# A hybrid decoder block on one core: w_out in program order, its weight tiles split one ahead, the Fox heads gated in pairs, ten modulation blocks within the attention

## The chip, the cores and the metric

One core of a Trainium2 chip runs the whole program. The metric is the device time of one execution in microseconds (us), the median of several. Engines: PE multiplies matrices, VectorE (DVE) and ScalarE (ACT) work element by element, GpSimd (POOL) does a little of the same and issues some DMAs, SyncE (SP) issues the other DMAs from one queue.

## What is computed

One decoder block for 512 tokens and model width 2048, in fp32. A vector c gives six modulation vectors; the hybrid mixer has eight forgetting-attention heads (Fox) and eight native-sparse heads (NSA); their outputs are normalised per group, scaled by beta, joined and multiplied by `w_out`; then comes a SwiGLU feed-forward.

```
mod = silu(c) @ w_ada + b_ada ; sh1, sc1, g1, sh2, sc2, g2 = split(mod, 6)
u   = rmsnorm(h) * (1 + sc1) + sh1 ; z = u @ w_in
y_f = rmsnorm(o_fox(z)) * beta_fox ; y_n = rmsnorm(o_nsa(z)) * beta_nsa
h   = h + g1 * (concat(y_f, y_n) @ w_out)
u   = rmsnorm(h) * (1 + sc2) + sh2
h   = h + g2 * ((silu(u @ w_gate) * (u @ w_up)) @ w_down) ; out = rmsnorm(h)
```

## The kernel before

Tiles have 128 rows. Each fp32 operand is split into a rounded high part and the rest (`wh`, `wl` for weights, `yh`, `yl` for a head's output), and a product is three matmuls (L278 to L280, or L283 to L285 where the activation is the stationary side): high by high, low by high, high by low.

**Weights.** `load_w` takes two rows of weight tiles ("a ct", 2 x 128 rows by 128 to 512 columns) through one ring of three raw tiles `wr`: SP loads it, ACT casts `wh` (L244), VectorE subtracts `wl` (L249). There are two `wh`/`wl` buffers; while there is a spare pool, every third tile goes to a further one, `wx`. `gemm` loads and splits a tile at each ct and then multiplies.

**The sides.** While `gemm` runs, `pump` advances side work by a step at each ct: `ada_block` (a modulation block of 512 columns: eight steps of one 512 KB load `ad` from the same ring of three and two VectorE operations each, L384 and L386; then eight one-column matmuls, L390), attention items (`att.run`) and, in the third and last pass over v, the NSA heads' gating `mix_chunk` (L947): the raw head `or` is reloaded (`reload`, L954, from a ring of five tiles), multiplied by the row scale (L948, on POOL for NSA heads and odd Fox heads, else VectorE), split into `yh` (ACT, L950) and `yl` (VectorE, L951). `mix_hook` pumps one step at ct 1 and two at each later ct. Nine modulation blocks are queued for the attention (L790), three remain.

**w_out.** Sixteen tiles of 128 output columns in groups of 4, 2, 4, 4, 2 columns (`g0`, `g1`, then groups 6, 10, 14, named by their first column). The sum runs over heads 8 to 15 (NSA, ct 0 to 3) and then 0 to 7 (Fox, ct 4 to 7). `g0` and `g1` do ct 0 to 3 first, with the attention's last items; the Fox heads are gated by `fox_hook` (L1024), two at each ct of `g1`; then ct 4 to 7 of `g0` and `g1` and the whole groups 6, 10 and 14 in the loop from L1193. At the end of a group `res_add` (L1061) adds to the residual `hT` and POOL stores it and sums squares. `x_hook` also loads the first feed-forward weights (`w_load`, L1076, `raw`) in group 10 and splits them (`w_sums`, `x_high`, `x_low`, `s_split`) in group 14.

**What sets the order.** SP runs in the program's order throughout. On the other engines a scheduler chooses the order until the feed-forward, where `tc.manual_schedule()` (L1231) makes them follow the program. A first pass, `z_qn` (L727), is followed by a v pass whose first tile `w_v0` is split ahead of the heads' rotations (L743).

Of the kernel before, what the change touches and what calls it, by code (L numbers as in the profile page):

```python
# [79 lines left out]
def hymba_block(ctx: ExitStack, tc: tile.TileContext, x, c, positions, w_ada, b_ada, norm_attn,  # L80
# [1111 lines left out]
    side_ada.extend(ada_block(pf, sec, j) for sec, j in todo_ada[9:])
    for i0, n, g in ((0, 4, g0), (4, 2, g1), (6, 4, BANKS_A), (10, 4, BANKS_B), (14, 2, BANKS_A)):  # L1193
        k0 = 8 if i0 < 6 else 0
        if i0 >= 6:
            g = out_group(i0, n, g)

        def x_hook(ct):
            if ct == k0 // 2 + 2:
# [4 lines left out]
            if i0 == 14:
                if ct == 2:
                    hsum["b"] = bank("s")
                    sum_tok(hsum, hsum["t"], True, False)
                if 1 <= ct < 3:
                    w_sums(ct - 1)
                if 1 <= ct < 4:  # L1210
                    x_high(ct - 1)
                if 1 <= ct < 5:
                    x_low(ct - 1)
                if 3 <= ct < 5:
                    s_split(ct - 3)
                if ct == 5:
                    w_sums(2)

        gemm(*g, order=order, k0=k0, hook=x_hook, n_ada=1)
        res_add(i0, [o[3] for o in g[3]], 2, hsum, "hsum")  # L1220
        for i in range(i0, i0 + n):
            nc.gpsimd.dma_start(hsd[i], hT[i])
# [204 lines left out]
```

## Time and profile before

| | |
|---|---|
| time, 3 runs | 2456.65, 2457.55 (median), 2460.13 us |
| the profiled execution | 2450.92 us, its span 2448.0 us |
| granted TensorE clock, mean | 0.981 of full |
| PE busy | 2355.1 us (96%) |
| VectorE, ACT, POOL busy | 65%, 42%, 14% |

All times below are counted from the span's start. PE is busy nearly throughout, so only its idle time, and the time that it runs at the lower granted clock, can change while its products stay the same. "Half clock" below is a granted clock of 0.50.

### The profile page before, as it was taken

How to read it: one execution, taken by the hardware profiler on the slowest of the kernel's cores; microseconds unless marked ns; L12 is line 12 of the kernel's file. 1: busy time of each engine (PE TensorE's matmuls, PEld its weight loads, DVE VectorE, ACT ScalarE, POOL GpSimd, SP SyncE). 2: the span in 40 equal slices, each digit the busy share in tenths (PEclk: the TensorE clock that was granted, in tenths of full speed). 3: DMA queues.
4: the chain of work that ended last, by engine and by line, in shares of the span. 5: the costliest groups of instructions: out<-in, count | busy, mean ns of one | idle time of the engine just before them, and what ended most of it. 6: DMA issues, size and time to landing. Idle time of an engine off the chain costs nothing.

```text
span 2448.0 us, 38482 instructions
## 1 busy us (share of the span) xinstructions
PE 2355.1 (96%) x14717; PEld 2100.4 (86%) x14717; DVE 1579.6 (65%) x2711; ACT 1016.0 (42%) x1531; POOL 341.5 (14%) x370
## 2 busy tenths in 40 slices
PE   6998999999999989889999999999999999999998
PEld 4677887888888767789999999999999888888887
DVE  6876786887755576596777777777776643333333
ACT  3224544344423332365555555555555422222133
POOL 0003002000001121251222121212221100000010
PEclk8998999999999999999999999999999999999999
DMA  9864743463554277559898989898988644333322
GB/s 332 283 198 147 205 139 95 130 190 117 180 174 129 85 249 253 186 122 237 211 231 215 228 213 232 220 225 212 221 200 193 192 151 141 123 120 121 102 95 101
DMA packets 322713, 440.31 MB, mean 180 GB/s; under 512 B 26224, under 2 KB 217552, under 8 KB 322528
## 3 DMA queue, kind: packets, MB, share of 16 engines
q1 hardware_dynamic: 289104, 348.21, 44.0%
q0 software_dynamic: 31120, 85.45, 18.7%
q10 hardware_dynamic: 2304, 4.20, 0.5%
q8 instruction: 115, 1.88, 0.3%
q14 instruction: 70, 0.57, 0.1%
HBM read 340.18 MB, written 28.38 MB: 151 GB/s over the span
## 4 chain that ended last, share of the span: by engine, by line
PE 54%; DVE 1%; DMA 0%; issue 0%; ACT 0%; SPq 0%; DVEq 0%; ACTq 0%
PE py L1161 12%; PE py L1164 11%; PE py L1163 11%; PE psmm L278 3%; PE psmm L279 3%; PE psmm L280 3%; PE pss L278 2%; PE pss L279 2%; PE pss L280 2%; PE pso L279 1%; PE pso L278 1%; PE pso L280 1%; DMA wr<-in_w_down_dram 0%; PE pso L1058 0%; DVE ul L1141 0%
## 5 line engine op out<-in xcount | busy, mean ns | idle before, releaser
L249 DVE TENSOR_TENSOR wl<-wr,wh 128x1024 fp32r<-128x1024 f32 (+2 forms) x211 | 239.0, 1133 | 381.5 <-ACT wh L244 378.4
L244 ACT CAST wh<-wr 128x1024 fp32r<-128x1024 f32 (+2 forms) x211 | 199.5, 948 | 502.7 <-PE psmm L279 199.7
L1164 PE MATMUL py<-uh,ls 128*128 128x256 f32 x1408 | 397.6, 282 | 3.6 <-DVE ls L1107 3.6
L1163 PE MATMUL py<-ul,hs 128*128 128x256 f32 x1408 | 397.6, 282 | 2.2 <-DVE ul L1141 2.2
L1161 PE MATMUL py<-uh,hs 128*128 128x256 f32 x1408 | 398.4, 283 | 1.0 <-DVE ev L1178 0.5
L1107 DVE TENSOR_TENSOR ls<-sum,hs 128x1024 fp32r<-128x1024 f32 x176 | 215.2, 1223 | 196.5 <-ACT hs L1101 196.5
L1101 ACT CAST hs<-sum 128x1024 fp32r<-128x1024 f32 x176 | 184.5, 1049 | 377.3 <-PE py L1163 257.5
L1163 PE MATMUL py<-ul,hx 128*128 128x256 f32 x1056 | 298.8, 283 | 4.0 <-DVE ul L1141 4.0
L1161 PE MATMUL py<-uh,hx 128*128 128x256 f32 x1056 | 299.3, 283 | 1.7 <-ACT uh L1140 1.4
L1164 PE MATMUL py<-uh,lx 128*128 128x256 f32 x1056 | 298.3, 282 | 0.0
L1164 PEld LDWEIGHTS py<-uh,ls 128*128 128x128 f32 x1408 | 267.0, 190 | 4.7 <-DVE ls L1107 4.6
L1163 PEld LDWEIGHTS py<-ul,hs 128*128 128x128 f32 x1408 | 267.0, 190 | 3.3 <-DVE ul L1141 3.3
L1161 PEld LDWEIGHTS py<-uh,hs 128*128 128x128 f32 x1408 | 267.1, 190 | 2.7 <-DVE ev L1178 1.3
L1097 POOL DMA_DIRECT2D lx<-raw x176 | 156.2, 887 | 580.2 <-ACT lx L1096 419.4
L1163 PEld LDWEIGHTS py<-ul,hx 128*128 128x128 f32 x1056 | 200.8, 190 | 5.1 <-DVE ul L1141 5.1
L1161 PEld LDWEIGHTS py<-uh,hx 128*128 128x128 f32 x1056 | 200.6, 190 | 2.2 <-ACT uh L1140 1.7
L1164 PEld LDWEIGHTS py<-uh,lx 128*128 128x128 f32 x1056 | 200.7, 190 | 0.0
L386 DVE SCALAR_TENSOR_TENSOR acc<-ad,sl,acc 128x512 f32<-128x512 f32 x180 | 141.6, 787 | 43.2 <-DMA ad<-in_w_ada_dram 41.4
L1092 ACT CAST hx<-raw 128x768 fp32r<-128x768 f32 x176 | 144.3, 820 | 11.3 <-DMA raw<-in_w_gate_dram 11.3
L1096 ACT ACTIVATE lx<-raw 128x768 fp32r<-128x768 f32 x176 | 148.1, 841 | 1.8 <-DMA raw<-in_w_gate_dram 1.8
L278 PE MATMUL psmm<-fh,wh 128*128 128x512 f32 x352 | 137.0, 389 | 0.0
L280 PE MATMUL psmm<-fh,wl 128*128 128x512 f32 x352 | 136.9, 389 | 0.0
(441 smaller groups left out, 5284.3 us busy)
## 6 DMA issues: line engine op xcount, KB each, us to landing
lx<-raw POOLq DMA_DIRECT2D x176, 384.0 KB, 5.2
ad<-in_w_ada_dram SPq DMA_DIRECT2D x128, 512.0 KB, 4.1
raw<-in_w_up_dram SPq DMA_DIRECT2D x176, 256.0 KB, 4.2
raw<-in_w_gate_dram SPq DMA_DIRECT2D x176, 256.0 KB, 4.5
wr<-in_w_down_dram SPq DMA_DIRECT2D x88, 512.0 KB, 3.6
ad<-in_w_ada_dram SPq DMA_DIRECT2D x128, 256.0 KB, 6.0
wr<-in_w_in_dram SPq DMA_DIRECT2D x104, 256.0 KB, 3.5
wr<-in_w_in_dram SPq DMA_DIRECT2D x24, 512.0 KB, 4.4
```

The source lines that it names most:

```text
L244: nc.scalar.copy(wh[:, :, sc], v)
L249: nc.vector.tensor_tensor(held[1][:, :, sc], v, split_ap(held[0])[:, :, sc], op=OP.subtract)
L278: nc.tensor.matmul(dst, wh[:, k, w], ah, start=first, stop=False)
L279: nc.tensor.matmul(dst, wh[:, k, w], al, start=False, stop=False)
L280: nc.tensor.matmul(dst, wl[:, k, w], ah, start=False, stop=last)
L1096: nc.scalar.activation(lx[s], raw[s][:, 1:4, :], AF.Copy, scale=-1.0)
L1097: nc.gpsimd.dma_start(split_ap(lx[s]), raw[s][:, 1:4, :], accum_op=OP.add)
L1101: nc.scalar.copy(hs[s], sums[s])
L1107: nc.vector.tensor_tensor(ls[s], sums[s], split_ap(hs[s]), op=OP.subtract)
L1161: nc.tensor.matmul(o, wh[:, wi, js], vh[:, vi, :], start=k == 0 and j == 0, stop=False, skip_group_check=True)
L1163: nc.tensor.matmul(o, wh[:, wi, js], vl[:, vi, :], start=False, stop=False, skip_group_check=True)
L1164: nc.tensor.matmul(o, wl[:, wi, js], vh[:, vi, :], start=False, stop=k == KG - 1, skip_group_check=True)
```

## The change

In the pass after `z_qn` the first two weight tiles are split ahead instead of one. Ten modulation blocks instead of nine are queued for the attention. `mix_hook` pumps one step per ct; what is left is pumped in `g0`. After the attention's last items every engine follows the program (`manual_schedule` begins there, not at the feed-forward). `load_out` loads and splits a tile one ct ahead of its `products`. The Fox heads are gated in pairs (`fox_pair`): four are reloaded at once, both products on VectorE, both `yh`, both `yl`, then the reload of the pair four further on. `res_add` of a group runs after the next group's first ct (`owed`), the first feed-forward weights are loaded at ct 3 to 7 of group 10 and ct 0 of group 14, and their splits are spread over ct 1 to 7 of group 14. Two modulation blocks remain for the loop, at set cts (`n_ada`).

```
-    w_v0 = z_qn(0, lambda: ahead(p_v0, extra=wsm), k0=ND // 2, ...)
+    w_v0 = z_qn(0, lambda: ahead(p_v0, extra=wsm) + ahead(p_v0, 1, extra=wsm), k0=ND // 2, ...)
-    side_ada.extend(ada_block(pa, sec, j) for sec, j in todo_ada[:9])
+    side_ada.extend(ada_block(pa, sec, j) for sec, j in todo_ada[:10])
-            pump(side_mix, 1 if ct == 1 else 2)
+            pump(side_mix, 1)
...
-    gemm(*g0, order=order, n_ada=1, n_att=1.25, k1=8)
+    def load_out(i0, ct):
+        return load_w(p_out[i0], order[2 * ct] // 2)
+    def products(g, ct, w):
+        gemm(*g, order=order, k0=2 * ct, k1=2 * ct + 2, first=[lambda: w])
+    gemm(*g0, order=order, n_ada=1, n_att=1.25, k1=8, hook=lambda ct: pump(side_mix, 2 if ct == 0 else 1000))
+    w1 = [load_out(4, ct) for ct in range(2)]
     att.drain()
-    rb = rows_of(sum_rstd(osum[0], FH * HD, "o", "rsf"), "o", q_tmp("rbf"))
-    def fox_hook(ct):
-        for h in fox[2 * ct:2 * ct + 2]:
-            mix_chunk(reload(h), h, rb)
-    gemm(*g1, order=order, n_ada=1, k1=8, hook=fox_hook)
     pump(side_ada, 1000)
+    ms.enter_context(tc.manual_schedule())
+    fox = {h: reload(h) for h in range(4)}
+    r = sum_rstd(osum[0], FH * HD, "o", "rsf")
+    products(g1, 0, w1[0])
+    rb = rows_of(r, "o", q_tmp("rbf"))
+    w1.append(load_out(4, 2))
+    products(g1, 1, w1[1])
+    def fox_pair(h):
+        for i in (h, h + 1):
+            nc.vector.tensor_tensor(fox[i], fox[i], rb, op=OP.mult)
+        for i in (h, h + 1):
+            y[i] = act_tile("y", i)
+            nc.scalar.activation(y[i][0], fox[i], AF.Copy, scale=beta[:, i:i + 1])
+        for i in (h, h + 1):
+            nc.vector.scalar_tensor_tensor(y[i][1], fox[i], beta[:, i:i + 1], split_ap(y[i][0]), ...)
+        if h + 5 < FH:
+            for i in (h + 4, h + 5):
+                fox[i] = reload(i)
+    fox_pair(0); w1.append(load_out(4, 3)); products(g1, 2, w1[2])
+    fox_pair(2); w0 = [load_out(0, 4)];     products(g1, 3, w1[3])
+    fox_pair(4); w0.append(load_out(0, 5)); products(g0, 4, w0[0])
+    fox_pair(6); w0.append(load_out(0, 6)); products(g0, 5, w0[1])
...
+        for ct in range(c0, 8):
+            if ct < 7:
+                nw = load_out(i0, ct + 1)
+            elif n_grp < 4:
+                nw = load_out(groups[n_grp + 1][0], starts[n_grp + 1])
+            pump(side_ada, ct in n_ada.get(i0, ()))
+            products(g, ct, w)
+            w = nw
+            if ct == c0 and owed is not None:
+                owed()
-            if i0 == 10 and 2 <= ct < 8:
-                w_load(ct - 2)
+            if i0 == 10 and ct >= 3:
+                w_load(ct - 3)
```

**SP around the Fox heads.** SP's queue from the load of `g1`'s ct 2 on, before: `or` are raw heads (from the third pair's first on), `wr` of 128x2x256 are tiles of `g1`, of 128x2x512 tiles of `g0`.

```order
L225 DMA wr_1541_8271<-in_w_out_dram 128x2x256
L956 DMA or_1544_8289<-osp_2480 128x512
L956 DMA or_1547_8296<-osp_2480 128x512
L225 DMA wr_1550_8303<-in_w_out_dram 128x2x256
L956 DMA or_1552_8320<-osp_2480 128x512
L956 DMA or_1555_8327<-osp_2480 128x512
L225 DMA wr_1558_8400<-in_w_out_dram 128x2x512
L380 DMA ad_1562_8407<-in_w_ada_dram 128x2x512
L225 DMA wr_1563_8435<-in_w_out_dram 128x2x512
```

And now, from the same load on:

```order
L225 DMA wr_1543_8280<-in_w_out_dram 128x2x256
L956 DMA or_1550_8308<-osp_2480 128x512
L956 DMA or_1551_8310<-osp_2480 128x512
L225 DMA wr_1552_8312<-in_w_out_dram 128x2x256
L956 DMA or_1558_8339<-osp_2480 128x512
L956 DMA or_1559_8341<-osp_2480 128x512
L225 DMA wr_1560_8343<-in_w_out_dram 128x2x512
L225 DMA wr_1567_8371<-in_w_out_dram 128x2x512
L225 DMA wr_1574_8411<-in_w_out_dram 128x2x512
```

In both, heads 4 and 5 stand before the load of `g1`'s ct 3, and heads 6 and 7 before that of `g0`'s ct 4; now no `ad` stands between the tiles of `g0`, and `g0`'s ct 4, 5 and 6 are called for back to back.

**ACT at the same place.** ACT's instructions from the row scale `rbf` on, before (`yh` is a head's high part, `wh` and `wx` are a weight tile's):

```order
L177 COPY rbf_1520_8199<-pso_1521_8200 128x512
L950 ACTIVATE yh_1527_8228<-or_1526_8225,vec_252 128x512
L950 ACTIVATE yh_1530_8235<-or_1529_8232,vec_252 128x512
L950 ACTIVATE yh_1536_8260<-or_1535_8257,vec_252 128x512
L950 ACTIVATE yh_1539_8267<-or_1538_8264,vec_252 128x512
L244 CAST wh_1542_8273<-wr_1541_8271 128x2x256
L950 ACTIVATE yh_1545_8292<-or_1544_8289,vec_252 128x512
L950 ACTIVATE yh_1548_8299<-or_1547_8296,vec_252 128x512
L244 CAST wx_1551_8305<-wr_1550_8303 128x2x256
```

And now:

```order
L177 COPY rbf_1541_8273<-pso_1542_8274 128x512
L244 CAST wh_1544_8282<-wr_1543_8280 128x2x256
L1046 ACTIVATE yh_1546_8300<-or_1534_8232,vec_252 128x512
L1046 ACTIVATE yh_1548_8303<-or_1535_8234,vec_252 128x512
L244 CAST wx_1553_8314<-wr_1552_8312 128x2x256
L1046 ACTIVATE yh_1554_8331<-or_1536_8236,vec_252 128x512
L1046 ACTIVATE yh_1556_8334<-or_1537_8238,vec_252 128x512
L244 CAST wh_1561_8345<-wr_1560_8343 128x1024
L1046 ACTIVATE yh_1563_8363<-or_1550_8308,vec_252 128x512
```

The cast of `g1`'s ct 2 moved from behind four heads to ahead of all, that of ct 3 from behind six heads to behind two, and that of `g0`'s ct 4 from behind ct 3's to between the second pair and the third. VectorE follows the same pattern.

**SP in group 10.** SP's queue from the first feed-forward weights (`raw`) on, before:

```order
L1080 DMA raw_1656_9084<-in_w_up_dram 128x2x256
L1081 DMA raw_1656_9084<-in_w_gate_dram 128x2x256
L225 DMA wr_1657_9087<-in_w_out_dram 128x2x512
L380 DMA ad_1660_9093<-in_w_ada_dram 128x2x512
L1080 DMA raw_1661_9121<-in_w_up_dram 128x2x256
L1081 DMA raw_1661_9121<-in_w_gate_dram 128x2x256
L225 DMA wr_1662_9124<-in_w_out_dram 128x2x512
L380 DMA ad_1665_9130<-in_w_ada_dram 128x2x512
```

And now, from the load just ahead of them:

```order
L225 DMA wr_1662_9107<-in_w_out_dram 128x2x512
L380 DMA ad_1665_9113<-in_w_ada_dram 128x2x512
L1115 DMA raw_1666_9141<-in_w_up_dram 128x2x256
L1116 DMA raw_1666_9141<-in_w_gate_dram 128x2x256
L225 DMA wr_1667_9144<-in_w_out_dram 128x2x512
L1115 DMA raw_1670_9174<-in_w_up_dram 128x2x256
L1116 DMA raw_1670_9174<-in_w_gate_dram 128x2x256
L225 DMA wr_1671_9177<-in_w_out_dram 128x2x512
```

A modulation load `ad` stood after every weight tile; now the last one stands ahead of the first `raw`.

## Rows read from the trace of the kernel before

**Rows 1.** The page: busy time, share of the span, instructions.
```profile
PE 2355.1 (96%) x14717; PEld 2100.4 (86%) x14717; DVE 1579.6 (65%) x2711; ACT 1016.0 (42%) x1531; POOL 341.5 (14%) x370
```

**Rows 2.** Stretches: us, busy time (count) per engine, granted clock, DMA share, GB/s.
```profile
224.20:234.40 10.20, 6.21 (x24) 5.86 (x25) 9.93 (x14) 5.17 (x11) 4.63 (x3) 0.50 0.42 130
692.66:717.15 24.49, 23.92 (x194) 23.30 (x194) 16.22 (x24) 3.37 (x6) 0.00 (x0) 1.00 0.70 209
779.17:810.45 31.28, 26.58 (x203) 26.08 (x203) 18.04 (x19) 12.10 (x18) 12.67 (x8) 0.89 0.36 119
797.60:804.40 6.80, 4.81 (x22) 4.51 (x22) 4.91 (x6) 2.48 (x4) 1.83 (x2) 0.50 0.35 110
890.68:906.95 16.27, 13.87 (x57) 10.79 (x56) 12.81 (x16) 5.18 (x8) 5.88 (x7) 0.90 0.82 279
906.95:951.54 44.59, 44.06 (x194) 35.95 (x194) 26.47 (x30) 10.64 (x12) 5.57 (x7) 1.00 0.74 244
951.54:1003.28 51.74, 48.20 (x210) 38.38 (x208) 34.68 (x44) 18.46 (x23) 11.46 (x14) 0.97 0.93 288
971.70:975.10 3.40, 3.40 (x9) 2.36 (x8) 3.37 (x6) 2.31 (x3) 0.87 (x1) 0.50 0.93 202
```

**Rows 3.** PE in order of time: start, us, line, [idle before <-releaser].
```profile
226.93 0.61 PE L283 MATMUL psmm<-wh,uh 128*128 128x288 f32 x1 [4.14 <-ACT wh L244]
...
797.40 0.43 PE L283 MATMUL psmm<-wh,uh 128*128 128x256 f32 x1 [2.71 <-ACT wh L244]
800.04 0.58 PE L285 MATMUL psmm<-wl,uh 128*128 128x256 f32 x1 [1.99 <-DVE wl L249]
...
852.13 1.96 PE L175 MATMUL pso<-cs,rsfr 128*128 128x128 f32 x8 [0.89 <-DVE rsfr L169]
859.59 0.50 PE L278 MATMUL pss<-yh,wh 128*128 128x512 f32 x1 [1.97 <-ACT wh L244]
867.59 0.50 PE L278 MATMUL psmm<-yh,wh 128*128 128x512 f32 x1
896.33 0.60 PE L280 MATMUL pss<-yh,wl 128*128 128x512 f32 x1 [2.32 <-DVE wl L249]
```

**Rows 4.** VectorE by form, 692 to 717 us: busy, mean ns of one.
```profile
L386 DVE SCALAR_TENSOR_TENSOR acc<-ad,sl,acc 128x512 f32<-128x512 f32 x15 | 11.3, 751 | 4.9 <-DMA ad<-in_w_ada_dram 4.5
L249 DVE TENSOR_TENSOR wl<-wr,wh 128x512 fp32r<-128x512 f32 x4 | 2.8, 688 | 1.6 <-PE psmm L285 1.0 <-ACT wh L244 0.6
```

**Rows 5.** VectorE, then POOL, in order of time, 786 to 800 us.
```profile
798.24 1.75 DVE L249 TENSOR_TENSOR wl<-wr,wh 128x512 fp32r<-128x512 f32 x1
...
786.76 12.67 POOL L948 TENSOR_TENSOR or<-or,rbn 128x512 f32<-128x512 f32 x8 [19.32 <-ACT rbn L177]
```

**Rows 6.** SP's queue in order of time; a long row is blocked.
```profile
774.76 15.45 SPq L956 DMA_DIRECT2D or<-osp  x2
...
851.64 7.52 SPq L956 DMA_DIRECT2D or<-osp  x2
860.68 0.42 SPq L225 DMA_DIRECT2D wr<-in_w_out_dram  x1
```

**Rows 7.** ACT in order of time at 859 and 866 us.
```profile
858.93 0.60 ACT L244 CAST wh<-wr 128x512 fp32r<-128x512 f32 x1
...
866.49 1.05 ACT L244 CAST wh<-wr 128x1024 fp32r<-128x1024 f32 x1 [2.06 <-DMA wr<-in_w_out_dram]
```

**Rows 8.** DMA issues: count, KB each, us to landing; issued at 858.8, 860.6, 955 to 990.
```profile
wr<-in_w_out_dram SPq DMA_DIRECT2D x1, 256.0 KB, 2.9
...
wr<-in_w_out_dram SPq DMA_DIRECT2D x1, 512.0 KB, 5.7
...
wr<-in_w_out_dram SPq DMA_DIRECT2D x6, 512.0 KB, 7.4
```

**Rows 9.** Who PE waited for in group 10: total, times, longest.
```profile
PE pss L278 <- ACT wh L244: 2.7, 2, 2.1
PE pss L280 <- DVE wl L249: 0.8, 2, 0.5
```

More of the change, by code (lines that the diff above doesn't have):

```diff
@@ L742, in hymba_block @@
     p_v0 = cols2(w_in, C_VS, 512, 2, P)
-    w_v0 = z_qn(0, lambda: ahead(p_v0, extra=wsm), k0=ND // 2, start=ND // 2, first=z_first)
+    w_v0 = z_qn(0, lambda: ahead(p_v0, extra=wsm) + ahead(p_v0, 1, extra=wsm), k0=ND // 2, start=ND // 2, first=z_first)
     nc.sync.dma_start(ca, cst[:, K_CM:])
@@ L1010, in hymba_block @@
         att.step()
-    pump(side_mix, 1000)
     def out_group(i0, n, tags):
         Z = [bank(t) for t in tags[:n]]
-        return [cols(w_out, i0 * P, n * P)], y, ND, [("ws", m * P, P, Z[m]) for m in range(n)]
+        return p_out[i0], y, ND, [("ws", m * P, P, Z[m]) for m in range(n)]
     order = list(range(8, 16)) + list(range(8))
-    g0 = out_group(0, 4, BANKS_A)
-    gemm(*g0, order=order, n_ada=1, n_att=1.25, k1=8)
-    att.drain()
-    rb = rows_of(sum_rstd(osum[0], FH * HD, "o", "rsf"), "o", q_tmp("rbf"))
@@ L1022, in hymba_block @@
-    fox = order[8:]
-    def fox_hook(ct):
-        for h in fox[2 * ct:2 * ct + 2]:
-            mix_chunk(reload(h), h, rb)
-    g1 = out_group(4, 2, BANKS_B)
-    gemm(*g1, order=order, n_ada=1, k1=8, hook=fox_hook)
-    pump(side_ada, 1000)
+    groups = [(0, 4, BANKS_A), (4, 2, BANKS_B), (6, 4, BANKS_A), (10, 4, BANKS_B), (14, 2, BANKS_A)]
+    p_out = {i0: [cols(w_out, i0 * P, n * P)] for i0, n, _ in groups}
+    def load_out(i0, ct):
+        return load_w(p_out[i0], order[2 * ct] // 2)
@@ new lines, in products @@
+    def products(g, ct, w):
+        gemm(*g, order=order, k0=2 * ct, k1=2 * ct + 2, first=[lambda: w])
+    g0 = out_group(*groups[0])
+    gemm(*g0, order=order, n_ada=1, n_att=1.25, k1=8, hook=lambda ct: pump(side_mix, 2 if ct == 0 else 1000))
+    w1 = [load_out(4, ct) for ct in range(2)]
+    att.drain()
+    pump(side_ada, 1000)
+    ms = ExitStack()
+    ms.enter_context(tc.manual_schedule())
+    fox = {h: reload(h) for h in range(4)}
+    r = sum_rstd(osum[0], FH * HD, "o", "rsf")
+    g1 = out_group(*groups[1])
@@ new lines, in hymba_block @@
+    products(g1, 0, w1[0])
[9 more added lines that the diff above has]
+        for i in (h, h + 1):
+            nc.vector.scalar_tensor_tensor(y[i][1], fox[i], beta[:, i:i + 1], split_ap(y[i][0]),
+                                           op0=OP.mult, op1=OP.subtract)
+        if h + 5 < FH:
+            for i in (h + 4, h + 5):
+                fox[i] = reload(i)
@@ L1031, in hymba_block @@
+    fox_pair(0)
+    w1.append(load_out(4, 3))
+    products(g1, 2, w1[2])
+    fox_pair(2)
+    w0 = [load_out(0, 4)]
+    products(g1, 3, w1[3])
+    fox_pair(4)
+    w0.append(load_out(0, 5))
+    products(g0, 4, w0[0])
+    fox_pair(6)
+    w0.append(load_out(0, 6))
+    products(g0, 5, w0[1])
     spare.clear()
@@ L1191, in hymba_block @@
     hsum = {"n": 14}
[L1192 to L1199, printed above, removed]
+    side_ada.extend(ada_block(pf, sec, j) for sec, j in todo_ada[10:])
+    w, owed = w0[2], None
+    starts = [6, 4, 0, 0, 0]
+    n_ada = {4: range(4, 8), 6: range(8), 10: range(4), 14: (2,)}
+    for n_grp, (i0, n, tags_) in enumerate(groups):
+        g = (g0, g1)[n_grp] if n_grp < 2 else out_group(i0, n, tags_)
+        c0 = starts[n_grp]
+        for ct in range(c0, 8):
[8 more added lines that the diff above has]
+                owed()
+            if ct == (7 if i0 == 0 else c0 + 2):
                 for i in range(i0, i0 + n):
                     nc.sync.dma_start(hT[i], xsp[i])
-            if i0 == 10 and 2 <= ct < 8:
-                w_load(ct - 2)
+            if i0 == 10 and ct >= 3:
+                w_load(ct - 3)
             if i0 == 14:
[L1205 to L1213, printed above, removed]
+                if ct == 0:
+                    w_load(5)
+                if ct in (1, 2, 5):
+                    w_sums({1: 0, 2: 1, 5: 2}[ct])
+                if ct in (1, 3, 5):
+                    x_high(ct // 2)
+                if ct in (2, 4, 6, 7):
+                    x_low((2, 4, 6, 7).index(ct))
                 if 3 <= ct < 5:
@@ L1216, in x_hook, with owed @@
                 if ct == 5:
[L1217 to L1222, printed above, removed]
+                    hsum["b"] = bank("s")
+                    sum_tok(hsum, hsum["t"], True, False)
+        def owed(i0=i0, n=n, g=g):
+            res_add(i0, [o[3] for o in g[3]], 2, hsum, "hsum")
+            for i in range(i0, i0 + n):
+                nc.gpsimd.dma_start(hsd[i], hT[i])
+    owed()
     pump(side_ada, 1000)
@@ L1230, in hymba_block @@
     aw.close()
-    ms = ExitStack()
-    ms.enter_context(tc.manual_schedule())
     kk = ExitStack()
```

## The prediction

> **What bounds the kernel now.** The page comes first: PE is busy 96% of the span, the next engine 65% [rows 1]. The change leaves PE's products as they are, so it can only win or lose PE's idle time and the time that PE runs at half clock. The table of stretches [rows 2] shows where there is any in what is touched, PE's own time line [rows 3] what ended each wait: on the matmuls of L278 to L285 always a weight tile's high part from ACT or its low part from VectorE. So each part below asks when a weight tile is split, and before that, when SP could issue its load.
>
> Two numbers serve throughout. A ct of two 128-row tiles costs PE 3.06 us in the v passes (24.49 us for eight [rows 2]) and in `w_out` about 5.4 us at four columns and 2.7 at two (44.59 us, less 0.5 idle and one L390 set, for eight of four columns). And half clock follows some waits: 797.6 to 804.4 (6.8 us) behind one of 2.71 us [rows 3], and 971.7 to 975.1 (3.4 us), are at 0.50 [rows 2]. A stretch of 3.4 us at half clock in which PE is busy gives 1.7 us of work away.
>
> **The first v pass.** Its second tile was cast behind the heads' rotations: PE waited 4.14 us at 226.93 [rows 3] and stood at half clock from 224.2 to 234.4, 10.2 us of which it was busy 6.21 [rows 2]. Split ahead, ct 1 follows ct 0 at once. But the cast and the subtraction (0.6 and 0.7 us) now stand ahead of the third head's rotation, whose later steps delay the third tile's split; VectorE was busy 9.93 of these 10.2 us, so its work, not the tile, ends the stretch. The wait moves from ct 1 to ct 2. I take -0.7 us; bounds -3 (half of the waits and the half clock's 3.1 us go) and +1 (the rotations 1.3 us later, little gained).
>
> **The third v pass, 779.17 to 810.45.** It took 31.28 us where the second took 24.49; with its eight L175 matmuls (0.8) some 6.0 us are lost. SP's queue stood still 15.45 us from 774.76, because two chunks a ct asked for more raw heads than the ring of five had free [rows 6]; the weight loads behind them came late, and PE waited 2.71 and 1.99 us [rows 3] and stood at half clock for 6.8. With one chunk a ct SP isn't blocked so. In return the tenth modulation block stands in this pass: eight loads of 512 KB on the same ring of three, and sixteen VectorE operations of 0.75 us [rows 4]. A ct then asks of VectorE 0.69 (`wl`), 1.5 (block) and 0.75 (`yl`, taken as the block's operation, which has its form) = 2.94 us if nothing slows it. POOL works 12.67 us on eight products, 1.58 each [rows 5], one a ct now, and beside it a `wl` took 1.75 instead of 0.69: over 1.58 us VectorE does about 0.7 us of work, so a ct costs 2.94 + 0.85 = 3.8 us against PE's 3.06. Eight of them are 30.3 us, and with L175's 0.8 this is 31.1: next to nothing. Some of it is hidden by the tiles split ahead: I take -1; bounds -6 (all that was lost) and +1.5 (the ring at 4 us a ct).
> By the Trainium skill (GPSIMD Engine Reference, 8. Key points) GpSimd and VectorE contend only where VectorE reads two SBUF inputs or is in a two-port mode. The block's operations read two, and the 1.75 us agree; were nothing slowed, the pass would need 25.3 us and the term be -6, which is the low bound anyway.
>
> **The attention's end.** `g1`'s ct 0 no longer fills the last items' waits but stands behind them, where it covers the row scale's chain (the 0.89 us wait at 852.13 [rows 3]). Work and cover trade places: 0, with L175 some 1.2 us later (twelve matmuls of 0.23, as 2.7 us a two-column ct, from 850.5 on end at 853.3).
>
> **The Fox heads.** This is the largest term, and it is a loss. SP's order is the same in both kernels: heads 4 and 5, `g1`'s ct 3, heads 6 and 7, `g0`'s ct 4. Head 5 waits for head 0's raw tile to be free, head 7 for head 2's (a ring of five). Before, all four `yl` of heads 0 to 3 came in one run, and `g0`'s ct 4 was called for at 860.68 [rows 6], cast at 866.49 [rows 7] and used at 867.59 [rows 3]. Now ACT and VectorE follow the program, and `g1`'s ct 3 stands between the pairs:
> - L175 853.3 to 854.9, `rbf` to 855.6, `wh` and `wl` of ct 2 to 856.8, two products (0.69 each) to 858.2, `yh` and `yl` of head 0 by 859.2.
> - Head 5 is issued then (before: 859.16, the end of the 7.52 us block [rows 6]), ct 3 at 859.6, landing in 2.9 us [rows 8] at 862.5; its split ends at 863.8.
> - Only then the products of heads 2 and 3 (865.2), `yh` and `yl` of head 2 (866.0). Head 7 is issued, `g0`'s ct 4 at 866.4 instead of 860.68.
> - That load took 5.7 us beside three others [rows 8]; beside one I take 4.9: 871.3, cast 1.05 [rows 7], 872.4. PE starts `g0`'s ct 4 there, 4.8 us later than at 867.59.
> PE has ended `g1`'s ct 3 at about 866, so it idles 6 us and more; half clock follows, 1.7 us. The first low product waits 0.5 for `wl`, and a later 0.5 us wait (885.5 us) goes as tiles are split ahead: 4.8 + 1.7 + 0.5 - 0.5 = +6.5. The 1.97 us wait at 859.59 [rows 3] goes too, but it lies ahead of the load that now decides. Bounds: +2 (the attention's end and the load each 2 us faster, no half clock) and +10 (5.7 us of landing, 6.8 us of half clock and a bit more).
>
> **The rest of `g1`, 16.27 us.** It has a wait of 2.32 us [rows 3] and 3.4 us of half clock. Now `res_add` of `g0` runs behind ct 4: four VectorE operations of 0.75 stand ahead of the split for ct 6, about 1.7 us late, and group 6's first tile can be called for only when the ring of three is free again, a ct late, 2.7. 10.9 us of products and those make 15.5 to 17.8 with or without half clock: +0.5, bounds -1 and +3.
>
> **Group 6:** its 0.5 us of idle goes: -0.5.
>
> **Group 10, 51.74 us** against 44.59 for the same products and one L390 set less. PE waits 2.7 and 0.8 us [rows 9] and has 3.4 us of half clock. The queue is full there: DMA share 0.93 at 288 GB/s [rows 2], tiles landing in 7.4 us [rows 8]. Now no modulation load stands beside the feed-forward's first weights, and POOL's transfers of their low parts move to group 14. The tiles land sooner, one ct ahead: 3.5 + 1.7 = -5.2; bounds -6.2 and -2.5 (one wait stays).
> The Trainium skill (DMA: Bandwidth & Descriptors, Issuing engines are not separate DMA queues) says that transfers of all engines end on the same 16 DMA engines, so POOL's are not free in group 14 either. The share of 0.93 with POOL's in it agrees. If they pushed out group 14's tiles as they did here, 2 us would come back, which is within the next term.
>
> **Group 14 and the start of the feed-forward.** Its tiles are of two columns, so a ct is 2.7 us, and the casts, low parts and sums are packed into them in the program's order; ct 2's tile is 0.5 to 1.4 us late behind them. +1; bounds 0 and +3. The L390 sets change places only: 0.
>
> **The sum:** -0.7 - 1 + 0 + 6.5 + 0.5 - 0.5 - 5.2 + 1 = +0.6 us. On the profiled execution's own 2450.92 this is 2451.5; the median of the runs stands 6.63 higher, 2457.55, and gives 2458.2.
>
> **The rivals.**
> 1. *The Fox loss is small and the v pass wins.* If POOL and VectorE don't meet (the chunks fall where VectorE has slack), the pass gives 6; if the attention ends earlier for want of filling and the tile lands in 3.5, Fox costs 2.5: -0.7 - 6 + 2.5 + 0.5 - 0.5 - 5.2 + 1 = -8.4, 2449. For it: the second v pass ran without waits with the same block in it. Against: that pass had no chunks.
> 2. *Slower: the tile behind head 7.* Three tiles of 512 KB are now called for back to back with head 7 just ahead. If they land as in group 10, 7.4 us, `g0`'s ct 4 starts 2.5 us later still, at 874.9, with 6.8 us of half clock (3.4): 7.3 + 3.4 + 0.5 - 0.5 = +10.7, and the sum is +4.8; with ct 5 late too, 2464. It decides from a landing after about 873. For it: 7.4 us [rows 8]. Against: the share there is 0.93 and here there is room.
> 3. *Splitting ahead does nothing,* as the ring and the queue set the pace: group 10 keeps half (-2.5), Fox costs only its bound of 2: -0.7 - 1 + 2 + 0.5 + 1 - 2.5 = -0.7, 2457, the same time for other reasons.
>
> **How the numbers follow.** Forecast 0.34, rival 1 0.30, rival 2 0.28, rival 3 0.08. A measurement of this kernel can tell 0.2%, 4.9 us, from no change. Rival 1 is faster (0.30), rival 2 slower (0.28), the rest the same (0.42). The range 2446 to 2467 takes in both outer cases with some 3 us beyond each; the forecast's own is 2453 to 2463.
>
> **What would show it.** Right: no blocked row of SP of 15 us near 780 and the v pass at 29 to 31 us; PE idle 5 to 7 us ahead of `g0`'s ct 4, its load issued about 13 us after the start of `rbf`'s L175; half clock after it; group 10 near 46 us at clock 1.00. Wrong: a load of `g0`'s ct 4 that lands before `g1`'s ct 3 ends (rival 1), VectorE idle over 10 us in the v pass, or `g0`'s ct 5 waiting as well (rival 2).

## The result and the profile after

The changed kernel took 2476.40 us (median of 4 runs, 2471.89 to 2478.08) against 2457.10 for the kernel before (4 runs, 2450.70 to 2460.13): a ratio of 1.0079, 95% interval 1.0055 to 1.0103. It is slower by 19 us (14 to 25). The forecast was 2458.2 and the range ended at 2467.

The page of the changed kernel, busy time by engine, answers to [rows 1]:

```profile
PE 2368.5 (96%) x14717; PEld 2111.5 (85%) x14717; DVE 1575.2 (64%) x2715; ACT 1014.6 (41%) x1531; POOL 335.5 (14%) x366
```

The two profiled executions are 28.0 us apart in span (2476.0 and 2448.0): the profile of before is of one of its fastest runs, that of the changed kernel of its slowest. The changed kernel's third v pass begins 14.4 us later, at 793.58 us for 779.17. Most of this is not the change: the nine kernels of this study with the changed kernel's code up to that pass began it between 782.3 and 794.0 us, and f4 below, which has the code of the kernel before up to there, at 788.3. So every stretch below is measured from the first product of one stage to the first product of the next, within one profile.

The stretches of the changed kernel, columns as in [rows 2]:

```profile
793.58:823.79 30.21, 27.57 (x214) 25.82 (x213) 25.91 (x33) 9.46 (x16) 8.64 (x7) 1.00 0.80 250
823.79:874.04 50.25, 44.27 (x198) 34.84 (x198) 23.13 (x55) 17.50 (x38) 4.45 (x3) 0.90 0.23 75
835.70:842.50 6.80, 4.95 (x14) 3.87 (x14) 6.76 (x13) 5.04 (x9) 0.00 (x0) 0.50 0.14 41
874.85:916.55 41.70, 34.73 (x136) 27.08 (x134) 17.36 (x23) 11.57 (x16) 0.00 (x0) 0.88 0.34 111
916.55:936.64 20.09, 14.46 (x50) 10.60 (x48) 10.53 (x14) 5.21 (x8) 6.33 (x7) 0.83 0.74 254
936.64:984.53 47.89, 46.71 (x201) 38.01 (x201) 26.16 (x30) 9.59 (x11) 3.61 (x4) 0.96 0.69 225
984.53:1031.88 47.35, 45.70 (x194) 37.01 (x193) 19.57 (x20) 10.42 (x13) 8.13 (x8) 0.96 0.73 244
1031.88:1063.81 31.93, 28.08 (x138) 23.00 (x136) 21.45 (x39) 15.69 (x24) 12.58 (x14) 0.95 0.67 182
```

And two of the kernel before that were not shown, the attention's end and the Fox heads' stretch:

```profile
810.45:852.13 41.68, 40.80 (x203) 32.17 (x201) 18.82 (x52) 15.53 (x35) 1.30 (x1) 1.00 0.15 46
853.74:890.68 36.94, 32.79 (x134) 24.94 (x134) 24.64 (x29) 12.52 (x17) 6.99 (x5) 0.97 0.66 209
```

| stretch, us | before | after | difference | forecast |
|---|---|---|---|---|
| first v pass, its first three cts (to L678) | 19.7 | 19.1 | -0.6 | -0.7 |
| third v pass | 31.3 | 30.2 | -1.1 | -1 |
| attention's end: `g0` to the Fox row scale, and to `g1`'s ct 1 | 43.3 | 51.1 | **+7.8** | 0 |
| Fox heads: `g1`'s ct 1 to its ct 4 | 36.9 | 41.7 | +4.8 | +6.5 |
| `g1`, ct 4 to 7 | 16.3 | 20.1 | **+3.8** | +0.5 |
| group 6 | 45.4 | 47.9 | **+2.5** | -0.5 |
| group 10 | 50.9 | 47.4 | -3.6 | -5.2 |
| group 14 and the start of the feed-forward | 30.5 | 31.9 | +1.5 | +1 |

From the third v pass on the differences add up to +15.7 us. The first line (72 products, up to L678, which is other work) took 18.6 to 19.4 us in the thirteen kernels with the new order there and 19.7 to 20.1 in the three with the old one. One profile of each kernel is not its mean: six kernels have the changed kernel's code up to the end of the attention (it, f1, f2, f3, h4, k3), and they took 30.2 to 31.4 us for the third v pass, 30.9 in the mean, and 50.2 to 53.3 us from `g0` to L175, 51.6 in the mean. The changed kernel's own profile has the lowest of both. So some 2 us of the 3.6 between the sum and the median's 19.3 lie in these two lines; the rest lies within the interval and was not located.

PE's longest waits of the changed kernel, to be read beside [rows 3] (`wx` is the spare tile):

```profile
833.79 0.41 PE L829 MATMUL pss<-cs,p 128*128 128x128 f32 x2 [1.53 <-DVE p L818]
...
838.61 0.79 PE L278 MATMUL psmm<-yh,wx 128*128 128x512 f32 x1 [1.85 <-ACT wx L244]
...
883.25 0.66 PE L278 MATMUL pss<-yh,wx 128*128 128x512 f32 x1 [2.69 <-ACT wx L244]
...
892.10 0.79 PE L278 MATMUL psmm<-yh,wh 128*128 128x512 f32 x1 [4.24 <-ACT wh L244]
...
924.74 0.80 PE L278 MATMUL pss<-yh,wh 128*128 128x512 f32 x1 [2.57 <-ACT wh L244]
...
936.64 0.50 PE L278 MATMUL psmm<-yh,wh 128*128 128x512 f32 x1 [2.87 <-ACT wh L244]
```

The first two lie in the attention's end, the next two at the Fox heads, the last two at the border of `g1` and group 6. The attention's end was at a clock of 1.00 before and is at 0.90 now: 835.7 to 842.5 is at half clock, which sets in between its two waits, and so is 869.8 to 873.2, behind two waits of 0.68 and 1.28 us among the last items.

### The profile page after: what moved, and what is told of

Same layout as the page of the kernel before. It is cut to its first block, busy times and chain, and to the rows that moved or that the text cites. A ratio compares the mean times of both kernels' runs of the same rounds, so it can differ in the third digit from the quotient of the medians.

```text
span 2476.0 us, 38462 instructions
## 1 busy us (share of the span) xinstructions
PE 2368.5 (96%) x14717; PEld 2111.5 (85%) x14717; DVE 1575.2 (64%) x2715; ACT 1014.6 (41%) x1531; POOL 335.5 (14%) x366
## 4 chain that ended last, share of the span: by engine, by line
PE 54%; DVE 1%; DMA 0%; issue 0%; ACT 0%; SPq 0%; DVEq 0%; ACTq 0%
PE py L1196 11%; PE py L1199 11%; PE py L1198 11%; PE psmm L280 3%; PE psmm L278 3%; PE psmm L279 3%; PE pss L278 2%; PE pss L279 2%; PE pss L280 2%; PE pso L280 1%; PE pso L279 1%; PE pso L278 1%; DMA wr<-in_w_down_dram 0%; DVE ul L1176 0%; PE pso L1093 0%
## 5 line engine op out<-in xcount | busy, mean ns | idle before, releaser
L386 DVE SCALAR_TENSOR_TENSOR acc<-ad,sl,acc 128x512 f32<-128x512 f32 x180 | 145.5, 809 | 31.3 <-DMA ad<-in_w_ada_dram 29.7
```

## The experiments

Each kernel is the changed one with the edit named, unless it says the kernel before. Times are medians beside runs of the kernel before on the same chip.

**e1: the gating as before.**

```
-            pump(side_mix, 1)
+            pump(side_mix, 1 if ct == 1 else 2)
...
+    pump(side_mix, 1000)
...
-    gemm(*g0, order=order, n_ada=1, n_att=1.25, k1=8, hook=lambda ct: pump(side_mix, 2 if ct == 0 else 1000))
+    gemm(*g0, order=order, n_ada=1, n_att=1.25, k1=8)
```

> The changed kernel with the NSA heads' gating put back as it was (two steps at each ct of the third v pass, the rest ahead of g0), ten modulation blocks kept. The stretch from g0's first product to the first L175 matmul of the Fox row scale took 41.7 us before and 50.3 us in the changed kernel. Theory A (the two gating chunks left for g0 push the split of g0's ct 1 back, so that attention items stand in a row on PE without products between them): the stretch comes back to 43 to 44.5 us, the third v pass grows from 30.2 to 31 to 33 us, and the run is about 2470 us or less, 4 to 7 us below the changed kernel. Theory B (the tenth block keeps the ring of three full, so that g0's tiles are loaded late): the stretch stays at 49 to 51 us and the run at 2474 to 2478.

The third v pass, then `g0` to L175, in e1:

```profile
785.95:823.52 37.57, 29.57 (x213) 28.35 (x212) 28.48 (x35) 11.19 (x18) 12.60 (x8) 0.86 0.68 215
823.52:869.41 45.89, 43.94 (x197) 34.35 (x198) 21.17 (x53) 16.53 (x36) 1.30 (x1) 0.93 0.22 71
```

2478.08 us, ratio 1.0073 (1.0057 to 1.0089). The attention's end won 4.4 us (50.25 to 45.89; 5.7 from the mean of the six), the way that theory A says though not down to its 43 to 44.5, but the v pass lost 7.4: with two steps at a ct and the tenth block in the same pass it is at clock 0.86. The forecast of the whole time for theory A was wrong for that reason.

**e2: nine blocks,** the third of the rest put into group 6, two steps at a ct.

```
-    side_ada.extend(... todo_ada[:10])
+    side_ada.extend(... todo_ada[:9])
...
-    side_ada.extend(... todo_ada[10:])
+    side_ada.extend(... todo_ada[9:])
...
-            pump(side_ada, ct in n_ada.get(i0, ()))
+            pump(side_ada, (2 if i0 == 6 else 1) if ct in n_ada.get(i0, ()) else 0)
```

> The changed kernel with nine modulation blocks within the attention instead of ten (the third of the rest goes into group 6, two steps a ct there). Theory A: the stretch from g0's first product to L175 stays at 48 to 51 us, because the two gating chunks are still left for g0; the third v pass falls from 30.2 to 26 to 28 us, group 6 is 1 to 3 us longer, the run 2473 to 2477. Theory B: g0's tiles are loaded some 8 us ahead again, the stretch falls to 42 to 44 us, and the run to 2466 to 2470.

The v pass, the attention's end and group 6 in e2:

```profile
782.52:807.61 25.09, 24.52 (x203) 24.11 (x203) 14.46 (x16) 9.61 (x15) 12.27 (x8) 1.00 0.52 157
807.61:857.66 50.05, 44.71 (x202) 35.40 (x201) 21.37 (x55) 17.70 (x38) 1.29 (x1) 0.90 0.18 59
920.51:978.26 57.75, 50.92 (x208) 41.25 (x209) 36.11 (x45) 9.56 (x10) 3.61 (x4) 0.91 0.74 240
```

2482.50 us, ratio 1.0094 (1.0075 to 1.0113). Theory B falls: the v pass is at 25.1 us, as good as without waits, so `g0`'s tiles are not late, and the attention's end still takes 50.05. What the tenth block cost in the v pass is 5.1 us. Two steps at a ct cost group 6 another 10 us (57.75) where 1 to 3 were expected, and so the run missed its forecast.

**e4: both,** gating and nine blocks as before.

> The changed kernel with both the gating and the nine blocks as before (the third of the rest in group 6, two steps a ct). All theories: the third v pass is as it was, 31 to 31.5 us. Theory A and theory B alike: the stretch from g0's first product to L175 is at 42 to 44 us (g1's ct 0 still stands behind the last items). If both theories are wrong and the loss comes from something else, the stretch stays over 47 us. The run 2468 to 2472.

2483.15 us, ratio 1.0094 (1.0078 to 1.0110): v pass 31.00, attention's end 44.29, group 6 60.64. The first is as expected and the second 0.3 us above its range; group 6 had e2's fault, and the run missed its forecast by it.

**e3: `g1`'s ct 0 free to stand in the attention's end.**

```
-    ms = ExitStack()
-    ms.enter_context(tc.manual_schedule())
     fox = {h: reload(h) for h in range(4)}
...
     products(g1, 0, w1[0])
+    ms = ExitStack()
+    ms.enter_context(tc.manual_schedule())
     rb = rows_of(r, "o", q_tmp("rbf"))
```

> The changed kernel with g1's ct 0 free to stand between the attention's last items again (the program's order begins behind it). Theory C (the twelve products that no longer fill the last items' waits are what the attention's end lost): the stretch from g0's first product to L175 falls from 50.3 by 2.3 to 3.5 us, and the run by as much, to 2473. Theory A: the products fill only the 0.7 and 1.3 us waits at the end, 1 to 2 us, while the bunched items ahead of them stay; the run 2474 to 2476.

2473.90 us, ratio 1.0062 (1.0047 to 1.0076); the stretch took 50.39 us, no less than 50.25. Alone, the missing fill is not the loss.

**h1: e1 and e3 together.**

> The changed kernel with the gating as before and g1's ct 0 free to stand in the attention's end, both at once (ten blocks kept, all else as changed). Alone, the first brought the stretch from g0's first product to L175 from 50.2 to 45.9 us and the second did nothing (50.4). Theory: the loss at the attention's end has these two parts, the leftover gating (which bunches the items) and, once that is gone, the missing fill; the stretch comes back to 41.7 to 42.7 us, and the third v pass stays at 37 to 38. Rival: something else in the change (the tenth block's tiles, the earlier split of g1's first two tiles) holds the rest: the stretch stays at 44.5 to 46 us.

The v pass, then `g0` to L175, in h1:

```profile
788.70:825.89 37.19, 29.66 (x214) 28.44 (x213) 28.45 (x35) 11.20 (x18) 11.95 (x8) 0.86 0.67 214
825.89:867.41 41.52, 40.64 (x198) 31.77 (x198) 21.12 (x53) 16.53 (x36) 1.30 (x1) 1.00 0.19 64
```

2477.25 us, ratio 1.0074 (1.0058 to 1.0090). The attention's end is back at 41.52 us (41.68 before) at clock 1.00, so these two edits are the whole of its loss: 4.4 us of leftover gating, and 4.4 more of fill, which only counts once the bunching is gone.

**f1: the load of `g0`'s ct 4 ahead of the reload of heads 6 and 7.**

```
-        if h + 5 < FH:
-            for i in (h + 4, h + 5):
-                fox[i] = reload(i)
+    def next_pair(h):
+        for i in (h, h + 1):
+            fox[i] = reload(i)
 
     fox_pair(0)
+    next_pair(4)
...
     fox_pair(2)
     w0 = [load_out(0, 4)]
+    next_pair(6)
```

> The changed kernel with one move in SP's queue: the load of g0's ct 4 stands ahead of the reload of Fox heads 6 and 7 instead of behind it. In the changed kernel that load went out at 886.5 us, some 7 us after g1's ct 3's, because head 7 waited for head 2's raw tile, and PE idled 4.24 us ahead of g0's ct 4. Theory: SP's queue is what makes g0's ct 4 late; the load goes out right behind g1's ct 3's, the 4.24 us wait and the half clock behind it go, and from g1's ct 1 to g0's ct 4 it takes 12 to 14 us instead of 17.25; the run 4 to 6 us below the changed kernel. Rival: the split of that tile stands behind two heads on ACT and VectorE anyway and the second pair's heads then come late: from g1's ct 1 to g1's ct 4 (41.7 us) no more than 1.5 us are won.

From `g1`'s ct 1 to its ct 4 in f1:

```profile
871.05:906.52 35.47, 32.07 (x135) 25.87 (x134) 17.36 (x23) 11.58 (x16) 0.00 (x0) 0.95 0.40 130
```

2471.47 us, ratio 1.0054 (1.0041 to 1.0066). The stretch fell from 41.70 to 35.47 us, below the 36.94 of before; to `g0`'s ct 4 it takes 13.54 instead of 17.25. The theory holds, the rival falls. Part of the 6.2 us was lost again behind it: `g1`'s ct 4 to 7 and group 6 took 20.9 and 50.4 us, 3.3 more than in the changed kernel.

**f2: `res_add` one ct later.**

```
-            if ct == c0 and owed is not None:
+            if ct == c0 + 1 and owed is not None:
```

> The changed kernel with a group's res_add one ct later (after the next group's second ct instead of its first). In the changed kernel four squares stood ahead of the cast for g1's ct 6 on ACT, and PE waited 2.57 us there. Theory 1 (the order of res_add and the split): that wait goes, g1's ct 4 to 7 fall from 20.1 to 17 to 18 us, the run 2 to 3 us below the changed kernel. Theory 2 (the tiles are late since SP stood still 9.6 us ahead of the loads of the residual): the tile for ct 6 comes no sooner, the wait moves to ct 7 or to group 6's first ct, and the two stretches, 20.1 and 47.9, add up to within 1.5 us of their 68.0.

2471.57 us, ratio 1.0059 (1.0046 to 1.0072): `g1` 18.29 and group 6 50.18, together 68.5 against 68.0. A wait of 3.83 us stands at ct 7 in place of the one at ct 6, as theory 2 says; group 10 took 44.3.

**f3: the spare pool given up one tile earlier.**

```
+    spare.clear()
     w0.append(load_out(0, 6))
     products(g0, 5, w0[1])
-    spare.clear()
```

> The changed kernel with the spare pool given up one tile earlier, so that g0's ct 6 no longer lies in the tile whose memory the residual's first load takes over. In the changed kernel SP waited 9.6 us for PE's last product of that ct, with g1's and group 6's tiles queued behind. Theory 2: SP's wait goes, g1's ct 5 to 7 and group 6's first tile are loaded some 8 us sooner, PE's waits of 2.87 us ahead of group 6 and the half clock go, and the two stretches of 20.1 and 47.9 us fall by 3 to 6 together; the run falls as much. Theory 1: the 2.57 us wait at g1's ct 6 stays, the two stretches fall by less than 2.

2471.45 us, ratio 1.0065 (1.0051 to 1.0079): 18.19 and 47.93, 1.9 us less than 68.0. PE's waits in f3 at `g1`'s ct 6 and ahead of group 6:

```profile
915.61 0.50 PE L278 MATMUL pss<-yh,wh 128*128 128x512 f32 x1 [0.76 <-ACT wh L244]
...
927.43 0.50 PE L278 MATMUL psmm<-yh,wh 128*128 128x512 f32 x1 [4.73 <-ACT wh L244]
```

SP's 9.6 us wait is gone and so is most of the wait at ct 6, but the one ahead of group 6 grew from 2.87 to 4.73. Neither theory is enough.

**h4: no modulation steps in `g1`'s ct 4 to 7,** but at every ct of groups 6 and 10.

```
-    n_ada = {4: range(4, 8), 6: range(8), 10: range(4), 14: (2,)}
+    n_ada = {6: range(8), 10: range(8), 14: (2,)}
```

> The changed kernel with no modulation steps in g1's ct 4 to 7 (they go to ct 4 to 7 of group 10). Theory 3 (the ring of three, shared with 512 KB modulation loads at every ct of 2.7 us, sets the pace there): g1's ct 4 to 7 fall from 20.1 to 15 to 17 us and group 6 from 47.9 to 45 to 46, group 10 rises from 47.4 to 49 to 51. Theory 2 alone (SP's wait for the spare tile): the fall is under 2 us in the two stretches together, as the tiles are called for late all the same.

`g1`, group 6 and group 10 in h4:

```profile
919.76:934.60 14.84, 13.07 (x50) 9.98 (x48) 7.65 (x8) 5.26 (x9) 6.36 (x7) 0.89 0.69 235
934.60:978.93 44.33, 44.33 (x202) 36.84 (x200) 23.25 (x26) 10.45 (x11) 3.62 (x4) 1.00 0.73 236
978.93:1023.69 44.76, 44.23 (x194) 35.97 (x194) 25.39 (x29) 9.55 (x12) 8.15 (x8) 1.00 0.85 275
```

2464.10 us, ratio 1.0021 (1.0009 to 1.0034): 5.3 and 3.6 us less, and two thirds of the whole loss gone with one line. Theory 3 holds for `g1` and group 6. The edit moves the block's VectorE operations and one-column matmuls along with its loads, so what the loads are worth alone is not shown. The forecast for group 10 failed: with a modulation load at every ct it fell to 44.76.

**k3: h4 with the low parts of the first feed-forward weights in group 10 again.**

```
+            if i0 == 10 and ct >= 4:
+                x_low(ct - 4)
...
-                if ct in (2, 4, 6, 7):
-                    x_low((2, 4, 6, 7).index(ct))
```

> The run without a block in g1 with one move: the low parts of the first feed-forward weights (ACT's copies and POOL's accumulating transfers) stand in group 10 at ct 4 to 7 again instead of in group 14. Before, group 10 took 50.9 us with these transfers and a modulation load at every ct; without the transfers, and with a modulation load at every ct, it took 44.8. Theory: POOL's transfers on the same DMA engines made the tiles late there; group 10 rises to 47.5 to 50 us and group 14 falls from 33.3 to 31 or 32. Rival: it was the order on ACT and VectorE (a tile split one ahead of its use); then group 10 stays within 1 us of 44.8.

Group 10 and group 14 in k3, and the landing of the tiles called for in group 10 (those of 256 KB are group 14's first):

```profile
968.48:1013.45 44.97, 44.39 (x194) 35.91 (x194) 23.93 (x27) 12.55 (x16) 10.74 (x11) 1.00 0.89 273
1013.45:1049.00 35.55, 29.76 (x137) 23.59 (x136) 22.80 (x41) 12.74 (x20) 9.91 (x11) 0.92 0.63 198
```

```profile
wr<-in_w_out_dram SPq DMA_DIRECT2D x5, 512.0 KB, 7.0
wr<-in_w_out_dram SPq DMA_DIRECT2D x3, 256.0 KB, 7.6
```

2465.64 us, ratio 1.0037 (1.0024 to 1.0051). Group 10 stayed at 44.97 us though its tiles land in 7.0 us, as late as before (7.4, [rows 8]). For group 10 the rival holds: it is the order in which a tile is called for and split. But the transfers were not free. Group 14, which the theory had falling to 31 or 32 us, rose from h4's 33.28 to 35.55: its first tiles landed in 7.6 us for 5.1 in h4, PE waited 1.84 us for the second of them, and 3.4 us at half clock followed. A ct is 2.7 us there.

**f4: the kernel before with the gating spread** (one step a ct, two from ct 6 on).

> The kernel before with one change: the gating of the NSA heads is one step a ct from ct 1 to ct 5 of the third v pass and two from ct 6 on, so that all eight heads are done in it (nine modulation blocks, w_out as before). If SP's blocked queue was what cost the pass 6 us, the pass falls from 31.3 to 25.5 to 28 us, g0's part stays at 41 to 43 us, and the run is 3 to 6 us faster than before. If the two steps at ct 6 and 7 push g0's first splits back as the leftover gating did in the changed kernel, g0's part grows by 3 to 8 us and the run is the same as before or slower.

2455.08 us, ratio 0.9990 (0.9981 to 0.9999). The v pass fell to 28.6 us (31.3), `g0`'s part stayed at 41.7: a gain of 2 us where 3 to 6 were expected, with a wait of 2.55 us left where two steps meet.

**h3: the kernel before with two steps at ct 3 and 5, and the tenth block's steps in the second and third q and k passes.**

> The kernel before with two edits: the gating spread in the third v pass (two steps at ct 3 and 5, else one, all eight heads in it), and the tenth block's steps in the second and third q and k passes, which leaves two blocks for w_out. Expected: v pass 25 to 28 us (31.3 before), attention's end as before (41.7), group 10 without modulation loads 46 to 48 us (50.9 before), so 6 to 9 us less than before, 2448 to 2451. If group 10's gain needs the later loads of the feed-forward's first weights as well, 50 us there and 3 to 4 us less in all.

2456.79 us, ratio 0.9999 (0.9988 to 1.0010). The v pass fell to 27.1 us, but group 10 took 52.8 without any modulation load, by one long wait:

```profile
968.99 0.80 PE L278 MATMUL pss<-yh,wh 128*128 128x512 f32 x1 [5.51 <-DVE mod L393]
```

PE's accumulator bank was still held by the last block's sums, whose reading (L393) stood on VectorE behind a sum that waited until 967.5 us for the feed-forward's raw weights, 9.3 us after their call. So modulation loads are not needed to make group 10 long, but it is another wait than the one of before.

**h2: what the runs pointed to, in one kernel:** two gating steps at ct 3 and 5, e3, f1, f3, h3's early block, two of `g1`'s modulation steps moved to `g0`.

> The changed kernel with what the runs point to: the gating done within the third v pass (two steps at ct 3 and 5, else one), g1's ct 0 free to stand in the attention's end, the tenth block's eight steps spread over the second and third q and k passes so that the third v pass has none, g0's ct 4 loaded ahead of Fox heads 6 and 7, the spare pool given up a tile earlier, and two of the modulation steps moved from g1 to g0. Expected from the stretches: v pass 25 to 28 us, attention's end 41.7 to 43, Fox 35.5 where before had 36.9, g1's ct 4 to 7 17 to 19, groups 6, 10 and 14 46, 46 and 31.5: some 8 us less than before, 2448 to 2452, if the early steps cost nothing in the q and k passes; the same as before if they cost 4 us each there.

2454.56 us, ratio 0.9987 (0.9976 to 0.9998): 3 us less than before where 8 were expected. v pass 27.5, attention's end 41.7, Fox 35.1, `g1` 12.3; group 6 took 50.2, which ate 4.8 us.

**k1: h2 with h4's line.**

> The combined kernel of h2 with no modulation steps in g0 and g1 (they stand in group 6 and group 10, one at every ct). In h2 the steps taken out of g1 left it at 12.3 us, but group 6 took 50.2. If modulation loads at 2.7 us a ct are the last cause of late tiles at that border, g1's ct 4 to 7 stay at 12 to 13 us, group 6 falls to 44.5 to 46 as in the run without a block in g1 (44.3), groups 10 and 14 stay within 1.5 us of 45 and 32.5: 4 to 6 us less than h2, about 2449, 0.3% faster than before. Rival: the wait ahead of group 6 moves to group 10's first tiles; the four stretches together, 140.2 us in h2, fall by less than 2.

Its v pass, attention's end, Fox heads, `g1`, group 6 and group 10:

```profile
789.48:816.62 27.14, 24.51 (x202) 24.11 (x202) 17.65 (x18) 11.99 (x18) 12.73 (x8) 1.00 0.45 138
816.62:858.33 41.71, 40.83 (x202) 32.16 (x201) 20.11 (x53) 15.63 (x35) 1.30 (x1) 1.00 0.16 51
859.22:894.15 34.93, 32.06 (x135) 25.72 (x134) 17.45 (x23) 11.81 (x17) 0.00 (x0) 0.95 0.55 178
894.15:905.93 11.78, 11.17 (x49) 8.93 (x48) 7.69 (x8) 5.34 (x9) 6.40 (x7) 1.00 0.45 139
905.93:950.26 44.33, 44.33 (x201) 36.85 (x200) 23.46 (x26) 10.39 (x11) 3.60 (x4) 1.00 0.76 251
950.26:994.75 44.49, 43.98 (x194) 35.99 (x194) 25.37 (x29) 9.57 (x12) 8.15 (x8) 1.00 0.84 274
```

2445.45 us (2441.08 to 2447.58) against 2458.44, ratio 0.9945 (0.9932 to 0.9957): 13 us faster than the kernel before and the best version of this study. The rival falls: group 6 is at 44.3 with no wait, group 10 at 44.5.

## Why the prediction was wrong, step by step

**The first v pass and the third** were right in size: -0.6 for -0.7, and -1.1 for -1 (-0.4 by the mean of the six). In the first, the wait moved from ct 1 to ct 2 as forecast: 4.14 us before [rows 3], 2.18 and 2.62 us at the third tile now (231.68 and 236.59). What the third pass would do follows from a table of two edits that the runs filled: nine blocks and two steps a ct 31.3 and 31.0 us (before, e4), nine and one 25.1 (e2), ten and two 37.6 (e1), ten and one 30.2 (after). Each edit alone is worth 5 to 7 us, and the change made both, with opposite signs. The prediction's -6 was the gating's half, and what it let the slowed VectorE take back, some 5 us, the block's. VectorE's block operations did get slower, 1.09 us each for 0.75 [rows 4]; whether they or the ring that they free set the pace (SP's tile loads stand 4.0 to 4.6 us apart there) was not separated.

**"Work and cover trade places: 0", the attention's end, is the step that failed.** It measured +7.8 us. I looked only at the twelve products of `g1`, and not at what the gating left over does. One step a ct over ct 1 to 7 is seven steps, and the row scale and eight heads need nine: two heads remain for `g0`. There the split of `g0`'s second tile stands on ACT behind them (ACT of the changed kernel in order of time):

```profile
834.50 0.72 ACT L950 ACTIVATE yh<-or,vec 128x512 fp32r<-128x512 f32 x1
...
836.23 0.72 ACT L950 ACTIVATE yh<-or,vec 128x512 fp32r<-128x512 f32 x1
...
837.52 1.04 ACT L244 CAST wx<-wr 128x1024 fp32r<-128x1024 f32 x1
```

That tile was cast at 837.5. PE's second and third L829 set of these items, in the kernel before (twelve products stand between them) and in the changed one (none do):

```profile
821.40 0.44 PE L829 MATMUL pss<-cs,p 128*128 128x128 f32 x2
...
825.76 0.49 PE L829 MATMUL pss<-cs,p 128*128 128x128 f32 x3
```

```profile
833.79 0.41 PE L829 MATMUL pss<-cs,p 128*128 128x128 f32 x2 [1.53 <-DVE p L818]
...
835.25 0.57 PE L829 MATMUL pss<-cs,p 128*128 128x128 f32 x3
```

The attention items now follow one another, each waiting for the other engines (1.53 us at 833.79, then 1.85 us for the tile itself), and half clock sets in. That the scheduler chose this order because it counted on the late tile is my reading; that the leftover gating and the missing fill bring the loss is shown: e1 takes out 4.4 us, h1 all of it. The prediction had moved `g1`'s ct 0 alone in PE's order.

**The Fox heads** were right in mechanism and close in size: +4.8, forecast +6.5. SP's queue in the changed kernel:

```profile
870.80 8.65 SPq L956 DMA_DIRECT2D or<-osp  x2
...
879.97 6.44 SPq L956 DMA_DIRECT2D or<-osp  x2
886.46 11.41 SPq L225 DMA_DIRECT2D wr<-in_w_out_dram  x5
911.30 1.76 SPq L1246 DMA_DIRECT2D hT<-xsp  x4
```

`g0`'s ct 4 was called for at 886.5, that is 12.4 us after L175's start at 874.04 (forecast 13); PE waited 2.69 us for `g1`'s ct 3 and 4.24 for `g0`'s ct 4. Counted from L175's start, `g0`'s ct 4 was forecast 3.6 us later than before (1.2 of the 4.8 are L175's own delay, which belongs to the attention's end) and came 2.6 later: the call came 0.7 us sooner than worked out, and the landing took 4.5 us for 4.9. f1 shows the cause by itself: the two reloads in front of it.

**The rest of `g1` and group 6, forecast 0 and measured +6.3,** is the second failed step. I put the late tile of group 6 at one ct, and left out what else was in the queue. (The terms given for `g1`, 10.9, 1.7 and 2.7, make 15.3 and not 15.5, which changes nothing.) Three things meet there. SP's wait for the residual's first load, whose memory was the spare tile's, in the changed kernel:

```profile
SPq L1246 <- PE psmm L280: 9.6, 1, 9.6
```

Before, that tile was last used by `g1`'s ct 3; splitting one ahead made `g0`'s ct 6 its last user, and SP stood with `g1`'s tiles behind (the hT row at 911.30 above). `res_add`'s squares ahead of ct 6's cast on ACT, its tile having landed at 920.12:

```profile
921.57 0.63 ACT L1082 ACTIVATE hsum<-hT 128x512 f32<-128x512 f32 x1 [2.84 <-DVE hT L1099]
922.23 1.95 ACT L1085 ACTIVATE sq<-hT 128x512 f32<-128x512 f32 x3
924.08 1.12 ACT L244 CAST wh<-wr 128x512 fp32r<-128x512 f32 x2
```

And, the largest, a modulation step at every ct of 2.7 us, its load going through the ring of three. Taking out the first (f3) or the second (f2) mostly moved the wait; taking out the third (h4) won 8.8 us in the two stretches.

**Group 10** won 3.6 us, forecast 5.2, for a wrong reason. I argued from fewer transfers in the queue. h4 and k3 put modulation loads and POOL's transfers back, and it took 44.8 and 45.0 us with tiles landing in 6.7 and 7.0 us. What differs is the order. Before, the tile of the longest wait (2.11 us at 971.09) was called for at 961.36, 7.6 us ahead of when PE wanted it, and landed at 968.57; ACT came to it 1.4 us later, behind the feed-forward's weights:

```profile
969.06 1.03 ACT L1101 CAST hs<-sum 128x1024 fp32r<-128x1024 f32 x1
970.00 1.04 ACT L244 CAST wh<-wr 128x1024 fp32r<-128x1024 f32 x1
```

In h4 ct 4's tile was called for at 990.83, 10.2 us ahead of its use, landed in 9.0 us and was cast at once; PE waited 0.5 us, for its low part. The changed kernel called for its own ct 4 9.0 us ahead and PE waited 1.13 us, with 3.4 us of half clock behind it, so group 10 stayed above the 46 us that the prediction named as its sign. k3's tiles, later with POOL's transfers than without (7.0 for 6.7 us, and 7.6 for 5.1), agree with the Trainium skill (DMA: Bandwidth & Descriptors, Issuing engines are not separate DMA queues), by which transfers started by any engine run on the same 16 DMA engines; what they cost fell on group 14.

**Group 14** was right, +1 and +1.5.

**The rivals.** The faster one fell: VectorE was busy 25.9 of the v pass's 30.2 us, and the Fox heads cost 4.8. The slower one was put at the landing of `g0`'s ct 4 after about 873 on the old clock; it landed 4.5 us after its call, so its mechanism did not occur. The kernel was slower by another. The third, a ring that sets the pace, was priced in group 10 and at the Fox heads; h4 points to it in `g1` and group 6.

## What to carry to other kernels

Count the steps of side work against the cts that pump it: what is left over runs in the next stage, ahead of that stage's first weights. A tile called for earlier hides a slow load: in group 10, with cts of 5.4 us, landings of up to 9.7 us cost 0.5 us of waiting in all (h4). Through cts of 2.7 us the same loads were late (`g1` here, group 14 in k3), so side loads belong into the long ones. Where a schedule is written anew, compare the order of the engine that bounds the kernel piece by piece, not only that of its helpers.
